# Weight sums of a quad made by accumulating loads, and more quads by seven products, in a decoder layer on one Trainium2 core

## The chip, the core and the metric

One core of a Trainium2 chip runs one launch of the kernel. The core has a matrix engine (TensorE, PE in the profile, with PEld for its weight loads), a vector engine (VectorE, DVE), a scalar engine (ScalarE, ACT), GpSimd (POOL) and SyncE (SP), each with an instruction queue of its own that runs in order, and 16 DMA engines that are shared by all queues that issue loads. The metric is the device time of one launch in microseconds; lower is better. Times are medians of several runs; the profile shows one execution.

## What is computed

One layer of a decoder trunk for 256 rows of 2048 numbers in float32: a modulation by a vector c, a large input projection, two mixers in parallel (a linear recurrence and a sliding-window attention), an output projection, and a SwiGLU feed-forward part with a hidden width of 5632, closed by a norm. The change touches the feed-forward part:

```python
h2 = modulate(rms_norm(x, norm2_g[l]), sh2, sc2)
gate, up = jnp.split(h2 @ w_ffn_in[l], 2, axis=-1)
x = x + g2 * ((jax.nn.silu(gate) * up) @ w_ffn_out[l])
return rms_norm(x, final_g)
```

## The kernel before

**Three products for one.** Every float32 product is taken as three products of rounded parts: each operand is split in a high part (a cast on ScalarE, "hi", line 305) and a low part (the difference on VectorE, "lo", line 317), and `mm3` (lines 353 to 357) issues high x high, high x low and low x high into the same bank. So a weight that was loaded by SP into a "raw" tile costs a cast and a subtraction before TensorE can use it.

**Items and queues.** The weights stream through a list of items, one 128x1024 piece each. `step(i)` (line 327) writes the program order: it issues the load for item i + 5, the high parts up to i + 3, the low parts up to i + 2, extra stages, and then the products of item i. There are five raw tiles, four hi tiles and three lo tiles, so a low part of item i + 2 can only be written after TensorE has finished item i - 1. Work beside the stream (posts, sides) is put between the items by estimated clocks; whatever is written for an engine is run in that order. `Item.before` holds stages that are issued just ahead of an item's products.

**The first FFN projection.** 11 slabs, each 512 columns of the gate half and 512 of the up half; a slab has eight pairs of k-tiles. Slab 0 runs plain, first its gate half (tile names fg), then its up half (fu). In slabs 1 to 10 (`add_pair`, line 1233) a pair of k-tiles, two row halves and two column halves is a 2x2 by 2x2 block product. A plain pair needs eight block products, 24 products of 128x512 with the three parts. A *quad* (`seven`, line 399) does the same with seven block products, 21 products, on sums of blocks: four sums on the side of the activations, made once, and four sums on the side of the weights, made on VectorE for each quad (lines 418, 419, 424, 425) into tiles named "made" or "last". Some of the seven results are shared by several outputs and are combined on VectorE at the end of a slab (`shared`, `gated_rows`). Before the change the pairs at k = 4, 8, 12 are quads (`SEVEN_1`).

**The last projection.** It runs over 44 k-tiles in two column halves, n = 0 and n = 2. In each half, eight pairs of the first 18 are quads (`SEVEN`), taken in turn with plain pairs (`turns`); the rest are plain. `seven_last` (line 1360) issues for each quad a cast "ah" and a difference "al" of the activation sums "fs"; `combined` adds the shared results.

**The gate row.** The second modulation's gate is made as a row: 32 VectorE operations (`ada_rows`, line 688) add products of loaded halves "aw" into "pa", then four TensorE products "pb" (line 694) sum it over the partitions and ScalarE copies it back. It runs as a side; `all_modulations`, a stage ahead of the first item of slab 1, finishes what is left of it. The halves "aw" use two tiles "araw", which in slabs 1 to 10 hold the weight sums.

Of the kernel before, what the change touches and what calls it, by code (L numbers as in the profile page):

```python
# [16 lines left out]
P = 128  # L17
# [26 lines left out]

N_K = 1
# [18 lines left out]
SEVEN = tuple(range(6, 36, 4))  # L64

SEVEN_1, SLAB_7 = (4, 8, 12), 1
EARLY = NH - 2 * N_HOLD

# [6 lines left out]
def hybrid_layer(  # L75
# [8 lines left out]
    hp = ctx.enter_context(tc.tile_pool(name="hp", bufs=1))  # L84
    bp = ctx.enter_context(tc.tile_pool(name="bp", bufs=N_B4))
# [13 lines left out]
    def b4(name, dt=F32, shape=(4, S)):  # L99
        used["b4"] += 1  # L100
        return bp.tile([P, *shape], dt, tag="b4", name=name)

# [174 lines left out]

    items = []
    live = {}
    at = {"load": 0, "made": 0, "hi": 0, "lo": 0}  # L280

    def do_load(i):
        src, cols = items[i].src, items[i].cols
        if callable(src):
            live[i] = [None, None, None, 0.0]
            return
        raw = wp.tile([P, CH], F32, tag="raw", name=f"raw{i}", bufs=AHEAD - 1)
        nc.sync.dma_start(raw[:, :cols], src)
        live[i] = [raw, None, None, load_time(cols)]

    def do_made(i):
        src = items[i].src
        if callable(src):
            clock["dve"] = max(clock["dve"], live[i - 1][3])
            live[i][0] = src(i)
            charge(1.2, 0)
            live[i][3] = clock["dve"]
# [29 lines left out]
    def step(i):  # L327
# [7 lines left out]
        if items[min(i + N_LO, len(items)) - 1].keep:  # L335
            run_posts()
        for stage in it.before:
# [58 lines left out]

    SUMS = 4

    def seven(loads, where, act, bank, begin, end, made_in, post=None):

        got = {}

# [8 lines left out]
        def block(k, n):  # L411
            l, c0 = where[k, n]
            return got[l][:, c0:c0 + 512]

        def first(i):
            got.update({0: live[i - 2][0], 1: live[i - 1][0]})
            x = got["x"] = made_in(0)
            nc.vector.tensor_tensor(x[:, 0:512], block(0, 1), block(0, 0), op=ALU.subtract)
            nc.vector.tensor_tensor(x[:, 512:], block(0, 1), block(1, 1), op=ALU.subtract)
            return x  # L420

        def second(i):
            y, x = made_in(1), got["x"]
            nc.vector.tensor_tensor(y[:, 0:512], block(1, 1), x[:, 0:512], op=ALU.subtract)
            nc.vector.tensor_tensor(y[:, 512:], block(1, 0), y[:, 0:512], op=ALU.subtract)
            return y

        plain = ((0, (0, 0), "p"), (1, (1, 0), "00"), (6, (1, 1), "01"))
        for l in range(2):
            jobs = [(a, where[kn][1], to) for a, kn, to in plain if where[kn][0] == l]  # L430
            cs = [c0 for _, c0, _ in jobs]
            items.append(Item(
                loads[l], CH, products(*jobs), weight=0.25 * len(jobs), used=(min(cs), max(cs) + 512),
            ))
        items.append(Item(first, CH, products((3, 0, "r"), (5, 512, "u")), weight=0.5))
        items.append(Item(second, CH, products((4, 0, "q"), (2, 512, "10")), post, weight=0.5))

    def sums_of(to, a11, a12, a21, a22):

        s1, s2, s3, s4 = (to[:, i, :] for i in range(SUMS))  # L440
        nc.vector.tensor_tensor(s1, a21, a22, op=ALU.add)
        nc.vector.tensor_tensor(s3, a21, a11, op=ALU.subtract)
        nc.vector.tensor_tensor(s2, s1, a11, op=ALU.subtract)
        nc.vector.tensor_tensor(s4, a12, s2, op=ALU.subtract)
# [63 lines left out]
    h_both = hp.tile([P, NK, 2, S], F32R, tag="h", name="h_both")  # L508
    h_hi, h_lo = h_both[:, :, 0, :], h_both[:, :, 1, :]

    def hact(kt):
# [4 lines left out]
        return h_hi[:, kt, :], h_lo[:, kt, :]  # L516
# [17 lines left out]
    def h_low(kt):  # L534
        nc.vector.tensor_tensor(h_lo[:, kt, :], hx[kt], f32(h_hi[:, kt, :]), op=ALU.subtract)
        h_done.add(kt)

    def modulated():
        for kt in range(2):
# [6 lines left out]
            nc.scalar.copy(h_hi[:, kt, :], hx[kt])  # L546
            yield 0.33, 0
            h_low(kt)
        for kt in range(2, NK):
# [6 lines left out]
            nc.scalar.copy(h_hi[:, kt, :], hx[kt])  # L556
# [540 lines left out]
    def second_norm(banks):  # L1097
        sides[:] = [ada_ffn]
        clock["slack"] = SLACK[1]
        both = h2["both"] = hp.tile([P, NK, 2, S], F32R, tag="h", name="h2_both")  # L1100
        hh, hl = both[:, :, 0, :], both[:, :, 1, :]
# [38 lines left out]
        def high(p):  # L1140
            for j in range(2):
                kt = 2 * p + j
                nc.scalar.activation(hh[:, kt, :], x1T[p][:, j, :], AF.Identity, bias=modc[:, 3, kt:kt + 1])

        def low(p):
            for j in range(2):
                kt = 2 * p + j
                nc.vector.scalar_tensor_tensor(
                    hl[:, kt, :], x1T[p][:, j, :], modc[:, 3, kt:kt + 1], f32(hh[:, kt, :]),
# [42 lines left out]
    def h2act(kt):  # L1192
        return h2["both"][:, kt, 0, :], h2["both"][:, kt, 1, :]
# [21 lines left out]
    def f_parts(s, pts):  # L1215
        if 4 * s + 2 not in SEVEN:
# [4 lines left out]

        fc, fs = b4(f"fc{s}", F32R, (2, 2, S)), b4(f"fs{s}", F32, (8, P))
        nc.scalar.copy(fc[:, 0], pts[0])
        nc.scalar.copy(fs[:, 0:2, :], pts[1][:, :, 0:P])
        nc.scalar.copy(fs[:, 2, :], pts[1][:, 1, P:])
        yield 0, 1.3
        nc.vector.tensor_tensor(fc[:, 1], pts[0], f32(fc[:, 0]), op=ALU.subtract)
        sums_of(fs[:, 3:7, :], fs[:, 0, :], fs[:, 1, :], pts[1][:, 0, P:], fs[:, 2, :])
        free(m=2)
        f_hi[s], f_lo[s], f_sum[4 * s + 2] = fc[:, 0], fc[:, 1], fs  # L1230
        yield 1.5, 0

    def add_pair(s):
# [24 lines left out]
        def shared():  # L1258
# [9 lines left out]
            nc.vector.tensor_tensor(x[:, 1, :], banks["r"], g[:, 1, :], op=ALU.add)  # L1268
            nc.vector.tensor_tensor(x[:, 0, :], banks["r"], x[:, 0, :], op=ALU.add)
# [19 lines left out]
        for k in range(0, NK, 2):  # L1289
            loads = [w_f1[s + 11 * n][:, k * 512:(k + 2) * 512] for n in range(2)]  # L1290
            if k in SEVEN_1:
                last = k == SEVEN_1[-1]
                seven(
                    loads, {(0, 0): (0, 0), (1, 0): (0, 512), (0, 1): (1, 0), (1, 1): (1, 512)}, act(k), bank,
                    k == SEVEN_1[0], last,
# [406 lines left out]
```

## Time and profile before

| | |
|---|---|
| median of 3 runs | 1551.02 us (1550.64 to 1556.88) |
| the profiled execution | 1549.47 us, of which the span from the first to the last instruction is 1547.7 |
| granted TensorE clock, mean | 0.997 |
| slab 0 of the first FFN projection | from 836.8 us of the span |
| slab 1 | from 884.1 us |
| last projection begins | about 1308 us |
| DMA queue of SP | 397.39 MB, 74.5% of 16 engines |
| DMA queue of GpSimd (software) | 1.06 MB |

A profile row names the line, the engine, the operation, the tile written and the tiles read, the shape, the count, then busy time and mean nanoseconds, and after the bar the idle time of the engine just before, with what ended it. In a timeline or chain row the first number is the start in the span and the second the duration. A busy TensorE is counted from modelled ends, so its products overlap: one takes some 390 ns and the next follows after some 227.

### The profile page before, as it was taken

The numbers are of one execution on the slowest core, as the hardware profiler recorded it, in microseconds if no ns is written. First come the engines' busy times: TensorE is split into PE (matmuls) and PEld (weight loads), VectorE is DVE, ScalarE is ACT, GpSimd is POOL, SyncE is SP. The second block draws the span as 40 slices with busy tenths as digits, with TensorE's granted clock in tenths as the row PEclk, the third lists the DMA queues.
The fourth block names the chain that finished last, engine by engine and source line by source line (L and its number), as shares of the span: only waits on it lengthen the run. The fifth ranks groups of instructions, "written<-read, shape, count | busy, mean of one in ns | idle before, by whom it ended". The sixth has DMA issues, their size and how long they took to land.

```text
span 1547.7 us, 22116 instructions
## 1 busy us (share of the span) xinstructions
PE 1530.9 (99%) x8013; PEld 1314.2 (85%) x8013; DVE 1392.2 (90%) x1854; ACT 858.2 (55%) x1113; POOL 3.7 (0%) x11
## 2 busy tenths in 40 slices
PE   8999999999999999999999999999999999999997
PEld 7999999998878887888888788888888888888786
DVE  7889989889888887988988899999999999998998
ACT  4654443776855445444545655555555556664664
POOL 0000000000000000000000000000000000000000
PEclk9999999999999999999999999999999999999999
DMA  9999998666887797999999665565555666766563
GB/s 367 343 320 345 341 315 291 212 203 208 270 275 264 259 328 274 368 339 339 366 384 346 191 202 187 194 198 200 200 192 200 207 193 236 251 206 204 189 212 128
DMA packets 112909, 400.37 MB, mean 259 GB/s; under 512 B 12432, under 2 KB 12576, under 8 KB 112416
## 3 DMA queue, kind: packets, MB, share of 16 engines
q1 hardware_dynamic: 112192, 397.39, 74.5%
q8 instruction: 62, 1.02, 0.3%
q0 software_dynamic: 320, 1.06, 0.2%
q10 hardware_dynamic: 288, 0.52, 0.1%
q14 instruction: 47, 0.39, 0.1%
HBM read 394.72 MB, written 4.20 MB: 258 GB/s over the span
## 4 chain that ended last, share of the span: by engine, by line
PE 93%; DMA 4%; DVE 2%; issue 1%; ACT 0%; SPq 0%; DVEq 0%; ACTq 0%
PE pf L1352 9%; PE f L356 7%; PE f L357 7%; PE f L355 7%; PE wi L357 6%; PE wi L355 6%; PE wi L356 6%; PE wga L357 2%; PE wga L355 2%; PE wga L356 2%; PE wa L357 2%; PE wa L355 2%; PE wa L356 2%; PE wl L356 2%; PE wl L357 2%; PE wl L355 2%
## 5 line engine op out<-in xcount | busy, mean ns | idle before, releaser
L305 ACT CAST hi<-raw 128x1024 fp32r<-128x1024 f32 (+1 forms) x540 | 536.9, 1002 | 447.3 <-PE wi L356 77.2
L317 DVE TENSOR_TENSOR lo<-raw,hi 128x1024 fp32r<-128x1024 f32 (+1 forms) x540 | 618.7, 1159 | 66.0 <-issue 35.0
L357 PE MATMUL wi<-h_both,lo 128*128 128x256 f32 x800 | 227.3, 284 | 3.6 <-DVE lo L317 3.6
L355 PE MATMUL wi<-h_both,hi 128*128 128x256 f32 x800 | 228.0, 285 | 0.0
L356 PE MATMUL wi<-h_both,hi 128*128 128x256 f32 x800 | 227.0, 284 | 0.0
L355 PE MATMUL f<-hi,h_both 128*128 128x512 f32 x460 | 180.2, 392 | 0.0
L357 PE MATMUL f<-hi,h_both 128*128 128x512 f32 x460 | 179.0, 389 | 0.0
L356 PE MATMUL f<-lo,h_both 128*128 128x512 f32 x460 | 179.0, 389 | 0.0
L357 PEld LDWEIGHTS wi<-h_both,lo 128*128 128x128 f32 x800 | 154.2, 193 | 4.0 <-DVE lo L317 4.0
L356 PEld LDWEIGHTS wi<-h_both,hi 128*128 128x128 f32 x800 | 154.3, 193 | 0.2
L355 PEld LDWEIGHTS wi<-h_both,hi 128*128 128x128 f32 x800 | 154.3, 193 | 0.2
L305 ACT CAST hi<-made 128x1024 fp32r<-128x1024 f32 x60 | 63.4, 1057 | 112.8 <-PE f L357 111.3
L496 DVE CUSTOM_DVE_ANT_0 aw<-aw,crow,vec 128x1024 f32<-128x1024 f32 x79 | 100.6, 1278 | 6.2 <-DMA aw<-in_ada_t_dram 6.2
L496 DVE CUSTOM_DVE_ANT_0 aw<-aw,crow,modc 128x1024 f32<-128x1024 f32 x79 | 100.9, 1280 | 3.0 <-DMA aw<-in_ada_t_dram 2.8
L357 PEld LDWEIGHTS f<-hi,h_both 128*128 128x128 f32 x460 | 86.3, 188 | 18.0
L355 PEld LDWEIGHTS f<-hi,h_both 128*128 128x128 f32 x460 | 86.4, 188 | 17.8 <-issue 0.2
L356 PEld LDWEIGHTS f<-lo,h_both 128*128 128x128 f32 x460 | 86.4, 188 | 17.8 <-issue 0.2
L317 DVE TENSOR_TENSOR lo<-made,hi 128x1024 fp32r<-128x1024 f32 x60 | 73.4, 1225 | 25.9 <-PE f L356 20.7
L1352 PE MATMUL pf<-hi,fc 128*128 128x512 f32 x256 | 71.0, 389 | 0.0
L305 ACT CAST hi<-last 128x1024 fp32r<-128x1024 f32 x32 | 33.7, 1054 | 52.5 <-PE pf L1352 49.2
L1352 PEld LDWEIGHTS pf<-hi,fc 128*128 128x128 f32 x256 | 48.1, 188 | 10.0
L355 PE MATMUL wl<-hi,yh 128*128 128x512 f32 x128 | 52.5, 410 | 0.0
(355 smaller groups left out, 2940.4 us busy)
## 6 DMA issues: line engine op xcount, KB each, us to landing
raw<-in_w_f_dram SPq DMA_DIRECT2D x176, 512.0 KB, 4.2
raw<-in_w_in_dram SPq DMA_DIRECT2D x164, 512.0 KB, 7.1
aw<-in_ada_t_dram SPq DMA_DIRECT2D x158, 512.0 KB, 6.5
raw<-in_w_f2a_dram SPq DMA_DIRECT2D x44, 512.0 KB, 4.3
raw<-in_w_f2d_dram SPq DMA_DIRECT2D x36, 512.0 KB, 3.4
raw<-in_w_lru_dram SPq DMA_DIRECT2D x32, 512.0 KB, 6.5
raw<-in_w_att_dram SPq DMA_DIRECT2D x32, 512.0 KB, 7.8
raw<-in_w_o_dram SPq DMA_DIRECT2D x32, 512.0 KB, 8.3
```

Source lines behind the costliest of these rows:

```text
L305: nc.scalar.copy(hi[:, cs], live[i][0][:, cs])
L317: nc.vector.tensor_tensor(lo[:, cs], raw[:, cs], f32(hi[:, cs]), op=ALU.subtract)
L355: nc.tensor.matmul(ps, lhsT=lh, rhs=rh, start=start, stop=False, skip_group_check=True)
L356: nc.tensor.matmul(ps, lhsT=lh, rhs=rl, start=False, stop=False, skip_group_check=True)
L357: nc.tensor.matmul(ps, lhsT=ll, rhs=rh, start=False, stop=stop, skip_group_check=True)
L496: nc.vector.tensor_tensor_reduce(out=r, in0=r, in1=crow[:, j * CH:(j + 1) * CH], op0=ALU.mult, op1=ALU.add, scale=1.0, scalar=dst if j els ...
L1352: nc.tensor.matmul(bank(t, n), lhsT=l[:, rows(t)], rhs=w[:, c0:c0 + 512], start=kt == 0 and k == 0, stop=kt == (EARLY - 2 if (t, n) == (1, ...
```

## The change

Two of a quad's four weight sums are no longer made on VectorE. GpSimd issues two *fill* loads of the same block into both halves of a tile "wx", and later two *adding* loads that add another block to each half while loading. VectorE makes the other two sums, "wy", from these (two operations instead of four). Signs are changed to make the additions possible. SP loads only the part of a block pair that a quad uses directly (three blocks of 256 KB instead of four). Fills are issued 11 items ahead, adds 8. With that, a slab has four quads instead of three (two in slab 10), in the order plain, plain, quad, quad, plain, quad, quad, plain; each half of the last projection has ten instead of eight, in the order of `TURNS`. `all_modulations` moves seven items ahead, so that "araw" is free for the fills. The activations h, the rows of the last norm and their gains move from one large tile into tiles of the pool "b4", which grows by eight.

```diff
+N_H = 8
...
-SEVEN = tuple(range(6, 36, 4))
-
-SEVEN_1, SLAB_7 = (4, 8, 12), 1
+
+N_SUM = (11, 8)
+SEVEN = (6, 10, 12, 14, 18, 22, 24, 26, 30, 34)
+
+SEVEN_1, SLAB_7, LAST_7 = (4, 6, 10, 12), 1, 2
+
+TURNS = "--77-77-77-77-77--"
 EARLY = NH - 2 * N_HOLD
+
+ALL_M = 7
...
-    hp = ctx.enter_context(tc.tile_pool(name="hp", bufs=1))
-    bp = ctx.enter_context(tc.tile_pool(name="bp", bufs=N_B4))
+    bp = ctx.enter_context(tc.tile_pool(name="bp", bufs=N_B4 + N_H))
...
+    def do_sum(j):
+        def do(i):
+            if items[i].sums is not None:
+                items[i].sums[j]()
+                load_time(CH)
+        return do
...
+        upto("fill", do_sum(0), i + N_SUM[0])
+        upto("add", do_sum(1), i + N_SUM[1])
...
+        def fill():
+            x = got["x"] = wp.tile([P, CH], F32, tag="araw", name="wx", bufs=N_ADA)
+            for j in range(2):
+                nc.gpsimd.dma_start(x[:, j * 512:(j + 1) * 512], block(0, 1))
+
+        def add():
+            for j in range(2):
+                nc.gpsimd.dma_start(got["x"][:, j * 512:(j + 1) * 512], block(j, j), accum_op=ALU.add)
 
         def first(i):
-            got.update({0: live[i - 2][0], 1: live[i - 1][0]})
-            x = got["x"] = made_in(0)
-            nc.vector.tensor_tensor(x[:, 0:512], block(0, 1), block(0, 0), op=ALU.subtract)
-            nc.vector.tensor_tensor(x[:, 512:], block(0, 1), block(1, 1), op=ALU.subtract)
-            return x
+            return got["x"], 0
 
         def second(i):
-            y, x = made_in(1), got["x"]
-            nc.vector.tensor_tensor(y[:, 0:512], block(1, 1), x[:, 0:512], op=ALU.subtract)
-            nc.vector.tensor_tensor(y[:, 512:], block(1, 0), y[:, 0:512], op=ALU.subtract)
-            return y
+            def raw(*kn):
+                l, c0 = where[kn]
+                return live[i - 3 + l][0][:, c0:c0 + 512]
+
+            y = b4("wy", F32, (CH,))
+            free(b4=1)
+            nc.vector.tensor_tensor(y[:, 0:512], got["x"][:, 0:512], raw(1, 1), op=ALU.add)
+            nc.vector.tensor_tensor(y[:, 512:], y[:, 0:512], raw(1, 0), op=ALU.add)
+            return y, 1.3
...
-        for k in range(0, NK, 2):
+        sevens = SEVEN_1 if s < 10 else SEVEN_1[:LAST_7]
+        others = [k for k in range(0, NK, 2) if k not in sevens]
+        for k in others[:2] + list(sevens[:2]) + others[2:3] + list(sevens[2:]) + others[3:]:
...
         if s == SLAB_7:
-            items[start].before.append(all_modulations)
+            items[start - ALL_M].before.append(all_modulations)
...
-            hi = parts[0] = wp.tile([P, 8, P], F32R, tag="araw", name=f"ah{n}_{k}", bufs=N_ADA)
+            hi = parts[0] = b4(f"ah{n}_{k}", F32R, (8, P))
...
-        others = [k for k in range(0, EARLY, 2) if k not in SEVEN]
-        turns = others[:2] + [k for two in zip(SEVEN, others[2:]) for k in two]
+        kinds = {"7": iter(SEVEN), "-": iter(k for k in range(0, EARLY, 2) if k not in SEVEN)}
+        turns = [next(kinds[c]) for c in TURNS]
```

VectorE, in the up half of slab 0, where the gate row is finished ("lo" a split of the weights, "pa" the gate row, "hs" sums of the activations). Before:

```order
L317 TENSOR_TENSOR lo_8376<-raw_8313,hi_8353 128x1024
L688 SCALAR_TENSOR_TENSOR pa<-aw_8015,cact,pa 128x1024
L317 TENSOR_TENSOR lo_8399<-raw_8333,hi_8374 128x1024
L688 SCALAR_TENSOR_TENSOR pa<-aw_8036,cact,pa 128x1024
L441 TENSOR_TENSOR hs_8414<-x1T_8168 128x128
```

And with the change:

```order
L339 TENSOR_TENSOR lo_8387<-raw_8324,hi_8364 128x1024
L721 SCALAR_TENSOR_TENSOR pa<-aw_8019,cact,pa 128x1024
L339 TENSOR_TENSOR lo_8410<-raw_8344,hi_8385 128x1024
L721 SCALAR_TENSOR_TENSOR pa<-aw_8040,cact,pa 128x1024
L721 SCALAR_TENSOR_TENSOR pa<-aw_8079,cact,pa 128x1024
L721 SCALAR_TENSOR_TENSOR pa<-aw_8190,cact,pa 128x1024
L721 SCALAR_TENSOR_TENSOR pa<-aw_8224,cact,pa 128x1024
L721 SCALAR_TENSOR_TENSOR pa<-aw_8251,cact,pa 128x1024
L721 SCALAR_TENSOR_TENSOR pa<-aw_8303,cact,pa 128x1024
L475 TENSOR_TENSOR hs_8442<-x1T_8179 128x128
```

The last six operations on pa, which stood between splits and sums up to the end of slab 0, now stand in one block.

TensorE, where the gate row's products pb stand, with the last rows of the item ahead and the first of the one behind. Before, between the up half of slab 0 (fu) and slab 1 (f):

```order
L356 MATMUL fu_0_1_8379<-lo_8484,h_both 128x512
L357 MATMUL fu_0_1_8379<-hi_8461,h_both 128x512
L694 MATMUL pb_8553<-pa,ones 128x512
L694 MATMUL pb_8556<-pa,ones 128x512
L694 MATMUL pb_8559<-pa,ones 128x512
L694 MATMUL pb_8562<-pa,ones 128x512
L355 MATMUL f_1_8565<-hi_8482,h_both 128x512
```

And with the change, behind the first of the eight items of the up half:

```order
L380 MATMUL fu_0_1_8390<-lo_8348,h_0_8093 128x512
L381 MATMUL fu_0_1_8390<-hi_8326,h_0_8093 128x512
L727 MATMUL pb_8418<-pa,ones 128x512
L727 MATMUL pb_8421<-pa,ones 128x512
L727 MATMUL pb_8424<-pa,ones 128x512
L727 MATMUL pb_8427<-pa,ones 128x512
L379 MATMUL fu_0_0_8389<-hi_8346,h_1_8094 128x512
```

The four products have moved ahead of seven items.

VectorE, one quad of the last projection ("al" the low part of its activation sums). Before:

```order
L418 TENSOR_TENSOR last<-raw_13241 128x512
L419 TENSOR_TENSOR last<-raw_13241,raw_13253 128x512
L317 TENSOR_TENSOR lo_13284<-raw_13241,hi_13267 128x512
L1370 TENSOR_TENSOR al_10_13286<-fs_9359,ah_10_13271 128x896
L424 TENSOR_TENSOR last<-raw_13253,last 128x512
```

And with the change:

```order
L339 TENSOR_TENSOR lo_13615<-raw_13571,hi_13601 128x512
L1422 TENSOR_TENSOR al_12_13617<-fs_9804,ah_12_13605 128x896
L456 TENSOR_TENSOR wy<-wx,raw_13586 128x512
L457 TENSOR_TENSOR wy<-wy,raw_13586 128x512
L339 TENSOR_TENSOR lo_13638<-raw_13586,hi_13613 128x1024
L339 TENSOR_TENSOR lo_13658<-wx,hi_13636 128x1024
L339 TENSOR_TENSOR lo_13665<-wy,hi_13656 128x1024
```

Two of the four sums are gone, and the first of the two left reads the tile wx, which GpSimd's loads fill.

More of the change, by code (lines that the diff above doesn't have):

```diff
@@ L101, in b4, with h_tiles @@
         return bp.tile([P, *shape], dt, tag="b4", name=name)
+    def h_tiles(name):
+        ts = [bp.tile([P, 2, 2, S], F32R, tag="b4", name=f"{name}{i}") for i in range(N_H)]
+        return [[ts[kt // 2][:, kt % 2, i, :] for i in range(2)] for kt in range(NK)]
     def sum_bank(name):
@@ L276, in __init__ @@
             self.used, self.before = slice(*(used or (0, cols))), list(before)
+            self.sums = None
     items = []
     live = {}
-    at = {"load": 0, "made": 0, "hi": 0, "lo": 0}
+    at = {"fill": 0, "add": 0, "load": 0, "made": 0, "hi": 0, "lo": 0}
+    def do_sum(j):
[4 more added lines that the diff above has]
+        return do
     def do_load(i):
@@ L397, in hybrid_layer, with seven @@
     SUMS = 4
-    def seven(loads, where, act, bank, begin, end, made_in, post=None):
+    def seven(loads, block, by_k, act, bank, begin, end, post=None):
         got = {}
+        where = {(k, n): (k, n * 512) if by_k else (n, k * 512) for k in range(2) for n in range(2)}
         def products(*jobs):
@@ L430, in seven @@
             jobs = [(a, where[kn][1], to) for a, kn, to in plain if where[kn][0] == l]
-            cs = [c0 for _, c0, _ in jobs]
+            cs = [where[kn][1] for _, kn, _ in plain if where[kn][0] == l]
+            used = (min(cs), max(cs) + 512)
             items.append(Item(
-                loads[l], CH, products(*jobs), weight=0.25 * len(jobs), used=(min(cs), max(cs) + 512),
+                loads[l][:, slice(*used)], CH, products(*jobs), weight=0.25 * len(jobs), used=used,
             ))
         items.append(Item(first, CH, products((3, 0, "r"), (5, 512, "u")), weight=0.5))
+        items[-1].sums = fill, add
         items.append(Item(second, CH, products((4, 0, "q"), (2, 512, "10")), post, weight=0.5))
@@ L1215, in f_parts @@
     def f_parts(s, pts):
-        if 4 * s + 2 not in SEVEN:
+        seven_ = [j for j in range(2) if 4 * s + 2 * j in SEVEN]
+        if not seven_:
             fh, fl = b4(f"fh{s}", F32R), b4(f"fl{s}", F32R)
```

138 lines of the change are left out of this document (75 added, 63 removed).

## The prediction

> **What bounds the kernel now.** I read the page first: busy time by engine, and the chain of work that ended last.
>
> ```profile
> PE 1530.9 (99%) x8013; PEld 1314.2 (85%) x8013; DVE 1392.2 (90%) x1854; ACT 858.2 (55%) x1113; POOL 3.7 (0%) x11
> ...
> PE 93%; DMA 4%; DVE 2%; issue 1%; ACT 0%; SPq 0%; DVEq 0%; ACTq 0%
> ```
>
> TensorE sets the time, VectorE is close behind, GpSimd is empty. Then the table by stage (columns: window, its length, busy time of PE, PEld, DVE, ACT, POOL, granted clock, DMA share, GB/s): a stretch of the output projections, one slab of the first FFN projection, and a stretch of the last projection.
>
> ```profile
> 600.00:800.00 200.00, 200.00 (x901) 165.26 (x900) 180.63 (x221) 93.74 (x120) 1.70 (x3) 1.00 0.98 350
> 974.86:1017.23 42.37, 42.37 (x193) 35.17 (x192) 39.36 (x49) 24.01 (x28) 0.00 (x0) 1.00 0.59 199
> 1334.00:1396.30 62.30, 62.30 (x277) 51.58 (x276) 60.36 (x68) 40.26 (x44) 0.00 (x0) 1.00 0.62 203
> ```
>
> In both changed stages TensorE has no gap at the full clock. VectorE fills 39.36 of 42.37 us and 60.36 of 62.30. The DMA engines are at about 0.6, and the first row shows that TensorE can be fed without a gap at 350 GB/s and share 0.98. The list of TensorE's waits names only these two in the last projection:
>
> ```profile
> PE pq L356 <- DVE lo L317: 0.2, 1, 0.2
> PE pr L356 <- DVE lo L317: 0.2, 1, 0.2
> ```
>
> So only fewer products, or a new wait, can move the end. The chain gives the price of a product: transposes recur once per slab, and 24-product pieces once per couple of one plain pair and one quad.
>
> ```profile
> 974.86 0.87 PE ft L957 x8
> ...
> 1017.23 0.87 PE ft L957 x8
> ...
> 1324.93 5.44 PE pf L1352 x24
> ...
> 1335.13 5.44 PE pf L1352 x24
> ```
>
> A slab takes 42.37 us, of which 0.87 are transposes; its 183 products take (42.37 - 0.87) / 183 = 0.2268 us each. A couple takes 10.20 us for 24 + 21 products, 0.2267 each; a plain pair is 5.44 us and a quad 4.76.
>
> **Fewer products.** A quad replaces 24 products of 128x512 by 21. Slabs 1 to 9 go from three quads to four, slab 10 from three to two: +8. The last projection goes from eight to ten in each of two column halves: +4. 12 x 3 = 36 products, 36 x 0.2267 = **-8.16 us**, all on the bound engine. Nothing else leaves TensorE.
>
> **The gate row is finished earlier.** VectorE makes the row "pa" in 32 operations, TensorE spreads it over the partitions in "pb". Before, pb stands at the head of slab 1; now it stands seven items earlier, after the first item of the up half of slab 0. Before this place the instructions stand as they did, so this trace dates it (VectorE, then TensorE):
>
> ```profile
> 855.73 2.36 DVE L317 TENSOR_TENSOR lo<-raw,hi 128x1024 fp32r<-128x1024 f32 x2
> 859.31 1.22 DVE L317 TENSOR_TENSOR lo<-raw,hi 128x1024 fp32r<-128x1024 f32 x1 [1.22 <-issue]
> 860.45 1.28 DVE L688 SCALAR_TENSOR_TENSOR pa<-aw,cact,pa 128x1024 f32<-128x1024 f32 x1
> 862.03 1.23 DVE L317 TENSOR_TENSOR lo<-raw,hi 128x1024 fp32r<-128x1024 f32 x1 [0.30 <-ACT x1T L1165]
> 863.17 1.28 DVE L688 SCALAR_TENSOR_TENSOR pa<-aw,cact,pa 128x1024 f32<-128x1024 f32 x1
> 864.37 0.28 DVE L441 TENSOR_TENSOR hs<-x1T 128x128 f32<-128x128 f32 x1
> ...
> 879.65 1.28 DVE L688 SCALAR_TENSOR_TENSOR pa<-aw,cact,pa 128x1024 f32<-128x1024 f32 x1
> ```
>
> ```profile
> 861.77 0.39 PE L357 MATMUL fu<-hi,h_both 128*128 128x512 f32 x1
> 862.00 0.39 PE L355 MATMUL fu<-hi,h_both 128*128 128x512 f32 x1
> ...
> 881.04 3.59 PE L694 MATMUL pb<-pa,ones 128*128 128x512 f32 x8
> ```
>
> Before, the last seven pa operations lie between the splits and end at 880.93; pb follows at 881.04 without a wait. Now six of them stand in one block behind the split of 862.03. That split needs the "lo" tile which the item ending on TensorE at 862.00 gives back (three tiles), so the block cannot begin before 863.17. The first column half of pa is complete after five operations. They follow one another every 1.20 us (863.17 to 864.37), so it is ready at 863.17 + 4 x 1.20 + 1.28 = 869.25. pb stands next in TensorE's queue from 862.0 on, and behind it all products of the up half: **+7.3 us** of an idle TensorE, whose inputs lie ready. Their being ready wins nothing back: no later part is bound by VectorE's lead. The 3.59 us of pb itself are the same as before. From below this wait is 0, if something finishes pa earlier; from above 8.5, if pb waits for the sixth operation too. I take 7.3, as both queues and the release are in these rows.
>
> **VectorE.** Durations in the last stretch:
>
> ```profile
> L317 DVE TENSOR_TENSOR lo<-raw,hi 128x1024 fp32r<-128x1024 f32 x20 | 23.8, 1219 | 0.0
> L418 DVE TENSOR_TENSOR last<-raw 128x512 f32<-128x512 f32 x6 | 4.1, 685 | 0.0
> ```
>
> Back to back an operation costs 0.08 less than its duration (two splits in 2.36 us: 1.14 to the next). A quad loses two of its four sums, 2 x 0.605; an added quad brings three more blocks to split and two sums. In a slab VectorE stays below 39.4 of now 41.7 us: hidden under TensorE. In the last projection the order becomes two quads, one plain pair. Two couples of before cost VectorE 60.36 / 62.30 x 20.40 = 19.76; less one plain pair (2.28) and four sums (2.42) that is 15.06 against TensorE's 2 x 4.76 + 5.44 = 14.96. Five double quads with four plain pairs between them are 73.0 against 69.4. The lead of two items shrinks from plain ones to quad ones (5.4 to 2.7 us) and covers 2.7 of the 3.6 missing, so about 0.9 us is lost in each half. With no lead it would be 3.6, with the spread of before 0: I take **+2** for both halves (0 to 7). ScalarE used 40.26 / 62.30 x 20.40 = 13.2 us in two couples and has less to cast in the new turn: hidden.
>
> **The accumulating loads.** Each quad now needs two fill loads and two adding loads of 256 KB from GpSimd's queue, the adds waiting for the fills, into two tiles in turn. The trace has no adding load; nearest are GpSimd's own loads and SP's.
>
> ```profile
> raw<-in_w_f_dram SPq DMA_DIRECT2D x176, 512.0 KB, 4.2
> ...
> raw<-in_w_f2a_dram SPq DMA_DIRECT2D x44, 512.0 KB, 4.3
> raw<-in_w_f2d_dram SPq DMA_DIRECT2D x36, 512.0 KB, 3.4
> ```
>
> ```profile
> L1021 POOL DMA_DIRECT2D g<-g1d x2: 527/541/555, 727.3 to 727.9; - x2
> ...
> DMA to landing us min/median/max: 5.4/7.2/10.0
> ```
>
> Call F the time from the first fill's issue to the landing of both, A the same for the adds. From SP's rows F = 4.3 + 0.54 for the second issue, about 4.9 at a DMA share of 0.6; from GpSimd's, issued at a share of 0.98, 7.2. A lies between the same ends, plus, if an add occupies the engines for twice its bytes, 0.5 MB / 350 GB/s = 1.5. A tile must do F, A, and then 3.5 us (two sums and two splits) per turn. In the last projection a turn is 14.96 us: **F + A up to 11.5 is hidden**. In a slab, the tile of the third quad comes free 1.2 us after TensorE begins the first quad (one split), and must be full 2.4 us (two sums and a split) before the second item of the third quad, which begins 2 x 4.76 + 5.44 + 1.36 = 16.3 us after the same moment: F + A = 12.7. GpSimd's queue holds fill, add, fill, add in turn, so the fourth quad's fill goes out only 1.2 + F + 1.1 after that moment; its deadline, 4.76 later, leaves 2F + A = 16.4. Three plain pairs in a row then restore the lead. I take F = 4.9 and A = 4.9 + 1.5 = 6.4 (F + A = 11.3, 2F + A = 16.2), since the demand stays short of saturation: a slab moves 44 blocks in 41.7 us, 277 GB/s. So I charge 0, with almost no reserve.
>
> The Trainium skill ("DMA: Bandwidth & Descriptors", Anatomy of one DMA) fits a GpSimd-issued load by 2.0 us plus its bytes over 436 GB/s; as an estimate, two loads of 256 KB together give 3.2, so F + A = 6.4 and no loss at all. The 7.2 us of this trace speak against it, though that was under load.
>
> **Sum.** 1549.47 (the profiled execution; span 1547.7) - 8.16 + 7.3 + 2 + 0 = 1550.6. The median of the runs shown, 1551.02, is 1.55 above that execution, so I forecast 1552.2.
>
> **Rivals.** Half a per cent, 7.8 us, is about what a measurement of this kernel can tell from no change.
>
> - The wait at pb is absent and only the products count: 1551.02 - 8.16 = 1543. For it: the inputs of pa landed long before. Against: both queues are in order. 0.09.
> - The tile is late (slower): the point is F + A = 11.5. At 7.2 + 7.2 each turn in the last projection takes 17.9, which is 2.9 too long, four times in each half: 23 us, 1575; at 12.5 it is 8 us, 1560. For it: two quads in a row put the DMA share near 0.96 (0.62 x 315 / 203), where 7.2 was seen. Against: TensorE waits first, and then demand falls. 0.23. If the slabs are late as well, 1.7 us for two quads in ten slabs add 34.
> - The engines' capacity: a turn moves 18 blocks, 4.72 MB, 315 GB/s; with every add counted twice 22 blocks, 5.77 MB, 385 GB/s. At 350 that takes 16.5 us, 1.5 too long, five times in each half: 15 us, 1567. 0.10. The Trainium skill states on the same page (Rules for kernel authors) that an accumulate reads its destination and writes it later; no run here shows what that costs.
>
> The forecast has the other 0.58. The range runs from 1546 to 1575: it leaves out the first rival (0.09) and the late slabs (about 0.08). Faster 0.09, within 0.58, slower 0.33 (both later rivals lie above 1558.8).
>
> **What would show it.** pb right after the first item of slab 0's up half, with a TensorE gap near 7.3 us before it; slabs of 42.37 - 0.68 = 41.69 us; two quads and a plain pair in 14.96; waits for "wx" on ScalarE and VectorE of about nothing. The forecast is wrong if pb does not wait, if slabs stretch over 42, or if the turn in the last projection follows the loads rather than 14.96.

## The result and the profile after

The change makes the kernel slower: 1602.62 us median against 1550.83, ratio 1.0334 [1.0307, 1.0361]; a second set of runs of the same kernel, the first of the experiments below, gave 1607.93 against 1551.80, 1.0366 [1.0334, 1.0397]. One of the four runs of the first set took 2566.84 us at a mean granted clock of 0.556, and one with plain loads below 2185.38 us at 0.654; the medians and ratios here leave these two out (with its run the first median is 1605.11). All rows of "after" are from a profiled execution of the second set (1611.21 us, span 1609.4).

The page after: TensorE has 36 products fewer, as counted, but its busy share falls from 99 to 96%, and loads of the sum tile "wx" stand in the chain that ended last.

```profile
PE 1546.9 (96%) x7977; PEld 1312.7 (82%) x7977; DVE 1382.7 (86%) x1825; ACT 877.4 (55%) x1146; POOL 172.5 (11%) x243
...
PE 77%; DMA 14%; DVE 4%; issue 2%; ACT 2%; POOL 1%; SPq 0%; DVEq 0%; ACTq 0%; POOLq 0%
DMA wx<-in_w_f_dram 7%; PE wi L381 6%; PE wi L379 6%; PE wi L380 6%; PE pf L1404 6%; PE f L379 5%; PE f L380 5%; PE f L381 4%; DMA wx<-in_w_f2d_dram 3%; DVE lo L339 3%; DMA wx<-in_w_f2a_dram 2%; PE wl L380 2%; PE wga L381 2%; PE wga L379 2%; PE wga L380 2%
```

Where the time went can be dated by the first and the last transposes "ft" of the slabs, in TensorE's timeline of before and of after.

```profile
889.95 1.03 PE L957 MATMUL ft<-ident,sg 128*128 128x128 f32 x8
...
1313.68 1.03 PE L957 MATMUL ft<-ident,v 128*128 128x128 f32 x8
```

```profile
901.77 1.03 PE L990 MATMUL ft<-ident,sg 128*128 128x128 f32 x8
...
1351.15 1.03 PE L990 MATMUL ft<-ident,v 128*128 128x128 f32 x8
```

Up to the first transposes after has lost 11.8 us; the ten slabs take 449.4 us instead of 423.7, 25.7 more; from there to the end of the span it is 258.2 against 234.0, 24.2 more. Since the 24 products fewer in the slabs should have saved 5.4 and the 12 fewer in the last projection 2.7, the losses are about 31 and 27 us. Two slabs and two stretches of the last projection by stage, and the list of TensorE's waits:

```profile
992.79:1041.36 48.57, 45.23 (x191) 36.10 (x189) 39.27 (x47) 25.40 (x30) 11.69 (x16) 0.93 0.82 239
1041.36:1085.47 44.11, 42.46 (x191) 34.39 (x189) 38.69 (x50) 25.20 (x31) 11.67 (x16) 1.00 0.88 261
1352.19:1438.32 86.13, 77.89 (x331) 62.70 (x331) 75.56 (x81) 54.24 (x62) 27.27 (x38) 0.98 0.91 272
1481.84:1567.34 85.50, 74.53 (x307) 58.80 (x307) 73.91 (x78) 52.05 (x58) 23.19 (x32) 0.96 0.84 243
```

```profile
PE pf L380 <- DVE lo L339: 18.9, 10, 3.4
PE f L380 <- DVE lo L339: 9.5, 9, 2.1
PE pb L727 <- DVE pa L721: 7.1, 1, 7.1
PE fr L380 <- DVE lo L339: 6.7, 10, 0.8
```

Before, TensorE stood without a gap in both stages. Now no engine is full there: TensorE waits 7.1 us once for the gate row (pb, in slab 0), 16.2 us in the slabs (f, fr) and 18.9 us in the last projection (pf) for low parts "lo". Where the gaps are long, the granted clock is under 1 as well (0.93 and 0.96), which adds to the loss. What the low parts wait for stands in the chain that ended last. This is its piece in the slab of 44.11 us (start, duration, engine, tile):

```profile
1052.69 1.83 DVE lo L339 x2
...
1054.81 5.78 DMA wx<-in_w_f_dram
...
1060.88 0.77 POOL wx L444
1061.65 7.64 DMA wx<-in_w_f_dram
1069.39 1.05 ACT hi L327
```

VectorE gives the sum tile back at 1054.52 with its split for the second quad; the fill goes out at once, the adds follow when the fill has landed, and ScalarE can cast the fourth quad's sums at 1069.39. The chain has such a piece in eight of the ten slabs. In the last projection ScalarE waits 23.9 us for sum tiles and VectorE 5.0. The loads say why the tiles are late (the fill loads, then the adding loads; "landing" is from issue to arrival):

```profile
L440 POOL DMA_DIRECT2D wx<-in_w_f_dram x76: 541/567/1125, 866.3 to 1296.1; - x76
...
DMA to landing us min/median/max: 2.8/5.9/9.7
```

```profile
L444 POOL DMA_DIRECT2D wx<-in_w_f_dram x76: 877/896/1240, 870.2 to 1304.4; - x76
...
DMA to landing us min/median/max: 3.8/6.6/9.9
```

Two fills take 0.57 + 5.9, about 6.5 us, and two adds 0.90 + 6.6, about 7.5: F + A = 14.0 us, beyond the limits of 11.5 and 12.7 that the prediction had worked out. In the piece above they take 14.8 (1054.52 to about 1069.3): 2.1 more than 12.7, in a slab that is 2.4 us longer than 41.7.

### The profile page after: what moved, and what is told of

It reads as the page before. It is cut to its first block, busy times and chain, and to the rows that moved or that the text cites. A ratio compares the mean times of both kernels' runs of the same rounds, so it can differ in the third digit from the quotient of the medians.

```text
span 2565.0 us, 22494 instructions
## 1 busy us (share of the span) xinstructions
PE 2547.5 (99%) x7977; PEld 1665.5 (65%) x7977; DVE 1416.1 (55%) x1825; ACT 898.4 (35%) x1146; POOL 172.9 (7%) x243
## 4 chain that ended last, share of the span: by engine, by line
PE 99%; DVE 0%; issue 0%; ACT 0%; DMA 0%; DVEq 0%; ACTq 0%
PE pf L1404 8%; PE f L379 7%; PE f L380 7%; PE f L381 7%; PE wi L380 6%; PE wi L379 6%; PE wi L381 6%; PE wl L380 2%; PE wga L379 2%; PE wa L379 2%; PE wgl L379 2%; PE wa L381 2%; PE wgl L380 2%; PE wo L381 2%; PE wgl L381 2%; PE wo L380 2%
## 5 line engine op out<-in xcount | busy, mean ns | idle before, releaser
L379 PE MATMUL wi<-h,hi 128*128 128x256 f32 x800 | 307.7, 385 | 0.0
L381 PE MATMUL wi<-h,lo 128*128 128x256 f32 x800 | 306.8, 384 | 0.0
L380 PE MATMUL wi<-h,hi 128*128 128x256 f32 x800 | 306.3, 383 | 0.0
L379 PE MATMUL f<-hi,h 128*128 128x512 f32 x412 | 239.2, 581 | 0.0
L380 PE MATMUL f<-lo,h 128*128 128x512 f32 x412 | 237.7, 577 | 0.0
L381 PE MATMUL f<-hi,h 128*128 128x512 f32 x412 | 236.7, 574 | 0.0
L379 PEld LDWEIGHTS wi<-h,hi 128*128 128x128 f32 x800 | 233.0, 291 | 1.4 <-issue 0.8
L380 PEld LDWEIGHTS wi<-h,hi 128*128 128x128 f32 x800 | 232.7, 291 | 1.3 <-issue 0.6
L381 PEld LDWEIGHTS wi<-h,lo 128*128 128x128 f32 x800 | 232.9, 291 | 0.1
L339 DVE TENSOR_TENSOR lo<-wx,hi 128x1024 fp32r<-128x1024 f32 x58 | 71.1, 1226 | 116.1 <-PE f L380 53.4
L381 PEld LDWEIGHTS f<-hi,h 128*128 128x128 f32 x412 | 90.8, 220 | 67.2 <-issue 37.0
L380 PEld LDWEIGHTS f<-lo,h 128*128 128x128 f32 x412 | 91.0, 221 | 66.4 <-issue 38.3
L379 PEld LDWEIGHTS f<-hi,h 128*128 128x128 f32 x412 | 89.8, 218 | 67.9 <-issue 39.6
L339 DVE TENSOR_TENSOR lo<-wy,hi 128x1024 fp32r<-128x1024 f32 x58 | 71.1, 1225 | 49.1 <-PE f L380 39.9
```

Source lines behind the costliest of these rows:

```text
L339: nc.vector.tensor_tensor(lo[:, cs], raw[:, cs], f32(hi[:, cs]), op=ALU.subtract)
L379: nc.tensor.matmul(ps, lhsT=lh, rhs=rh, start=start, stop=False, skip_group_check=True)
L380: nc.tensor.matmul(ps, lhsT=lh, rhs=rl, start=False, stop=False, skip_group_check=True)
L381: nc.tensor.matmul(ps, lhsT=ll, rhs=rh, start=False, stop=stop, skip_group_check=True)
```

## The experiments

Three theories stood at first. **Theory 1**: the tile is late, because two tiles in turn don't give fill, wait and add enough time. **Theory 2**: the 16 DMA engines are full, with the adds counted twice. **Theory 3**: VectorE is too full in the last projection. The runs' edits are against the changed kernel unless said; the kernel before gave medians of 1551.7 to 1552.8 us beside them.

**The change again.**

> The changed kernel as it is, for a profile at the full clock. Theory 1 (the sum tile wx comes too late: fill, wait, add, and only two tiles): TensorE waits some 7 us for the gate row and in all some 45 us for splits of wx and wy, in the slabs (about 43 to 45 us each instead of 41.7) and in the turns of the last projection (16 to 18 us instead of 15.0); SP's own loads land as before (4 to 5 us) and ScalarE waits for wx, not for raw. Theory 2 (the DMA engines are full): the DMA share is above 0.95 in the slabs, SP's loads land in 7 us or more and ScalarE waits for raw as much as for wx. Theory 3 (VectorE is full in the last projection): VectorE has no idle time in the turns and the loss lies there alone.

1607.93 us; its rows are those above. Slabs take 43.2 to 48.6 us and turns 16.9 to 18.7, with ScalarE waiting for wx, as theory 1 had it, at a share of 0.82 to 0.88 in the two slabs shown; but SP's loads land later too (a median of 5.1 us in the slabs and 6.7 in the first half of the last projection, against 4.2 and 4.3 before).

**Plain loads in place of the adding ones** (the weight sums are not computed), in two runs:

```diff
-                nc.gpsimd.dma_start(got["x"][:, j * 512:(j + 1) * 512], block(j, j), accum_op=ALU.add)
+                nc.gpsimd.dma_start(got["x"][:, j * 512:(j + 1) * 512], block(j, j))
```

> The second loads of each quad no longer add, they overwrite the first (so the two weight sums are not computed). Same bytes from HBM, same queues, same waits. Theory 1, with the add as the long part: the second loads land as fast as the fills and most of the loss goes: about 1565 us or less. Theory 2: if an add counts twice in the engines, the time falls as well, with the DMA share; if not, it stays near 1603. Theory 3: stays near 1603.

> The change with plain loads in the place of the accumulating ones, once more for a profile at the full clock (the weight sums are not computed). If the accumulating load itself is what takes long, the second loads land in the time of the fills, 5.9 us or less, and GpSimd issues them in 0.57 us instead of 0.90, so F + A falls from 14 to about 12 and slabs to about 42.5. If GpSimd's queue or the full engines make both long, the second loads take 6.6 us here too.

1572.33 us, 1.0134 [1.0116, 1.0151], and 1573.02 in the single later run: 35 us of the loss go with the addition alone, somewhat less than theory 1 had expected. The fills, the second loads, and a slab of the later run:

```profile
L440 POOL DMA_DIRECT2D wx<-in_w_f_dram x76: 536/538/543, 865.1 to 1269.8; - x76
...
DMA to landing us min/median/max: 2.7/4.3/7.3
```

```profile
L444 POOL DMA_DIRECT2D wx<-in_w_f_dram x76: 536/538/547, 869.1 to 1276.5; - x76
...
DMA to landing us min/median/max: 2.8/4.8/7.4
```

```profile
1070.70:1112.67 41.97, 41.97 (x189) 34.45 (x188) 38.46 (x47) 25.48 (x30) 8.56 (x16) 1.00 0.79 276
```

Without the addition a pair of fills takes 4.3 + 0.54 = 4.84 us, almost exactly the F = 4.9 of the prediction, and the second pair 5.3: together 10.2, under both limits, and slabs come down to between 42.0 and 43.1 (eight full ones; 42.4 on average). The addition makes the second loads longer by 1.8 us in landing and 0.36 in GpSimd's issue of each, and it makes the fills beside them longer too, by 1.6. The turns of the last projection still take mostly 16.1 us here, though its tiles come in time.

**Three sum tiles instead of two** (a third 4 KB tile, one tile fewer in the ring b4):

```diff
-AHEAD, N_HI, N_LO, N_ADA, N_B4 = 6, 4, 3, 2, 25
+AHEAD, N_HI, N_LO, N_ADA, N_B4 = 6, 4, 3, 3, 25
...
-    bp = ctx.enter_context(tc.tile_pool(name="bp", bufs=N_B4 + N_H))
+    bp = ctx.enter_context(tc.tile_pool(name="bp", bufs=N_B4 + N_H - 1))
...
-                if self.own < N_ADA:
+                if self.own < 2:
```

> Three tiles for wx instead of two (the gate row's halves still use two of them; the pool b4 has one tile less). A fill need no longer wait for the quad before last. Theory 1: the turn per tile grows by half, so the loss beyond the gate row's wait mostly goes: 1555 to 1565 us. Theory 2 and theory 3: near 1603.

1569.66 us, 1.012 [1.0103, 1.0137], above the 1555 to 1565 expected. The adds land as late as before (6.6 us), but the slabs take 42.0 to 42.1 us (transposes at 1022.77 and 1064.84) and the waits "f" are gone but for 0.2 us: in the slabs theory 1 is shown. The last projection stays long; its turn of two quads and a plain pair takes 16.8 us instead of 14.96 in the first half, and 16.1 to 17.5 in the second.

Some 5 us of what this run gains on the change lie ahead of the first FFN projection, where no quad is at work. The first product of that projection starts at 833.2 us, in the change at 838.4; in all runs with three tiles it starts between 831.8 and 833.5, in those with two, the kernel before included, between 836.8 and 838.4. No run tells why.

**The old counts and order with the accumulating loads** (three quads in a slab, eight in each half of the last projection, in turn with plain pairs):

```diff
-SEVEN = (6, 10, 12, 14, 18, 22, 24, 26, 30, 34)
+SEVEN = tuple(range(6, 36, 4))
-SEVEN_1, SLAB_7, LAST_7 = (4, 6, 10, 12), 1, 2
+SEVEN_1, SLAB_7, LAST_7 = (4, 8, 12), 1, 3
-TURNS = "--77-77-77-77-77--"
+TURNS = "--7-7-7-7-7-7-7-7-"
...
-        for k in others[:2] + list(sevens[:2]) + others[2:3] + list(sevens[2:]) + others[3:]:
+        for k in range(0, NK, 2):
```

> The accumulating loads with the old numbers and the old order of quads (three per slab at k = 4, 8, 12, eight per half, always with a plain pair between two quads). 36 more products than the change: +8.2 us. Theory 1: a tile's turn is 20.4 us (two couples) and fill plus add fit in it: 1551 + 7 = about 1558 us, the wait for the gate row alone. Theory 2: three quarters of the extra bytes: about 1590. Theory 3: VectorE has 2 x 0.6 us less per quad than in the kernel before: about 1558.

1561.85 us, 1.006 [1.0043, 1.0078]. A slab, two couples of the last projection, and its wait at pb:

```profile
1070.11:1112.48 42.37, 42.37 (x193) 35.18 (x191) 36.02 (x43) 23.99 (x28) 8.77 (x12) 1.00 0.85 255
1354.73:1375.13 20.40, 20.40 (x92) 16.90 (x91) 17.61 (x20) 13.06 (x15) 5.83 (x8) 1.00 0.93 283
```

```profile
870.40 5.87 PE L727 MATMUL pb<-pa,ones 128*128 128x512 f32 x8 [7.13 <-DVE pa L721]
```

Slabs and couples take the 42.37 and 20.40 us of before, so in both stages the accumulating loads as such cost nothing when quads stand apart, at 283 GB/s and a share of 0.93; VectorE even does with 17.61 us where it had 19.76. Nearly all of the loss that is left stands at pb, in a wait of 7.13 us and products that then take 5.87 instead of 3.59; these 2.3 us were not in the 1558 expected.

**Four quads in the slabs, the last projection in its old order, two tiles** (only the lines SEVEN and TURNS of the diff above):

> The change, but the last projection again with eight quads that alternate with plain pairs (the old order); the slabs keep four quads. Two sum tiles, as in the change. Theory 1 (with two sum tiles, fills and adds of two quads in a row are not done in time, F + A about 14 us against limits of 12.7 in a slab): the slabs are long again, 43.8 to 48.6 us, and the waits for the tile stay there, about 31 us more than nine slabs of 41.7; the last projection is as before, couples of 10.2 us. Sum: before 1551.8 + 7.1 (pb) - 10 slabs x 0.68 + 31 = 1583, 1578 to 1590. Theory 2 (DMA engines full): much of the loss comes from the last projection's two adjoining quads, so under 1570. If the slabs alone make the loss, 1600 or more.

1586.08 us, 1.0221 [1.0201, 1.024]. As theory 1 had it: the slabs are long again (ten take 449 us), so they lose by themselves, TensorE waits nowhere in the last projection, and theory 2's account, in which most of the loss comes from the adjoining quads there, falls.

**The last projection: three tiles, its rows loaded later.** In the run with three tiles VectorE's timeline showed a wait in each turn of the first half:

```profile
1362.99 0.69 DVE L456 TENSOR_TENSOR wy<-wx,raw 128x512 f32<-128x512 f32 x1 [0.57 <-PE pf L380]
```

The second sum "wy" of the second quad waits for a tile of the ring b4 that TensorE still reads for the first quad, and what is behind it on VectorE waits too. (The run with plain loads, which has the tile more in this ring, does not show this wait.) So the rows x2 and fg, which hold three tiles of that ring for each half, were loaded late:

```diff
-                last_first()
-                sides.append(Side(fetch_last()))
+                last_first()
+            if jobs[0][0] == ROWS_AT and jobs[0][1] in (0, 2):
+                sides.append(Side(fetch_last(jobs[0][1] // 2)))
...
+ROWS_AT = 20
```

> Three sum tiles (as in the run with three), and the rows x2 and fg of the last projection, three 4 KB tiles for each half, are loaded at k-tile 20 of their half instead of at its beginning, so that up to then three to six more tiles of the ring b4 are free there. Nothing else moves. Theory A (in the run with three tiles the turn of two quads and a plain pair took 16.77 us instead of 14.96 because the second quad's sum tile wy, from the ring b4, waits for the end of the first quad, which reads the tile ah: VectorE stands, and with it the split of the next plain block): turns of 15.0 to 15.2 us up to k-tile 20, 1569.7 - 8 turns x 1.7 = about 1556, 1553 to 1559. Theory B (VectorE or the DMA engines are full at two quads and a plain pair, 281 GB/s with each add counted once): turns stay at 16.5 to 16.8, 1568 to 1571.

1567.42 us, 1.0099 [1.0083, 1.0115]: a miss for theory A, mostly. The wait is gone, but the turn only falls to 16.1 us. One turn of VectorE, ScalarE and TensorE (single lines), and two turns by stage:

```profile
1355.52 1.23 DVE L340 TENSOR_TENSOR lo<-wx,hi 128x1024 fp32r<-128x1024 f32 x1 [0.69 <-issue]
1357.05 1.23 DVE L340 TENSOR_TENSOR lo<-wy,hi 128x1024 fp32r<-128x1024 f32 x1 [0.30 <-ACT hi L328]
```

```profile
1353.20 1.06 ACT L328 CAST hi<-wx 128x1024 fp32r<-128x1024 f32 x1 [1.66 <-PE pf L1403]
1355.96 1.06 ACT L328 CAST hi<-wy 128x1024 fp32r<-128x1024 f32 x1 [1.71 <-PE pf L1403]
```

```profile
1354.82 0.61 PE L1403 MATMUL pf<-lo,fc 128*128 128x512 f32 x2
```

```profile
1346.28:1362.40 16.12, 15.27 (x66) 12.31 (x67) 15.06 (x17) 10.94 (x13) 5.79 (x8) 1.00 0.96 279
...
1378.55:1394.65 16.10, 15.25 (x66) 12.31 (x66) 15.05 (x17) 10.94 (x13) 4.32 (x6) 1.00 1.03 364
```

VectorE is busy 15.06 us of each turn, the predicted figure, and idle for 1.0. While TensorE does the plain pair (its two pieces last 2.72 us each), buffers come back slowly, and VectorE waits twice. The wait of 0.69 us is not for a cast: the cast of wx ended at 1354.26. It ends at 1355.52, just after the last products that read the plain pair's second low part (1354.82 + 0.61), so what is missing there is a lo tile, of which there are three. The wait of 0.30 is for the cast of wy, which itself had waited 1.7 us for a hi tile. 15.06 + 1.0 is the turn. The second row is the turn in which the rows were loaded as well: 364 GB/s, and the same length. So the DMA engines don't set it, and theory 2 and theory B's DMA part fall. Theory 3 holds for the last projection, in the form that VectorE's work and its waits fill the turn. In the second half the late rows cost a step of 4.1 us: VectorE waits 3.2 us and ScalarE 6.3 for a sum tile whose loads went out among theirs.

**pb at the head of slab 1, on top of that** (`row_made` finishes pa; `all_modulations` then issues pb):

```diff
...
-            items[start - ALL_M].before.append(all_modulations)
+            items[start - ALL_M].before.append(row_made)
+            items[start].before.append(all_modulations)
```

> As the run before it, and the gate row pa is still finished seven items early, but its four products pb go out at the head of slab 1, as in the kernel before; so TensorE's wait of 7.1 us at pb should be gone. Expected: 6 to 7 us less than the run with the rows later: 1549 by theory A (1546 to 1552), 1563 by theory B. If pb's wait was covered by another wait right behind it, the two runs are equal.

1563.52 us (1556.33 to 1569.35), 1.0071 [1.0045, 1.0098]. The wait at pb is gone, and all slabs start 4.5 us earlier (1017.32 instead of 1021.84), not 6 to 7: in its place TensorE waits 2.0 us once for a low part of slab 0 ("fu"), and the next products run at half the pace for some 3 us. The spread of these runs is as large as the gain; the slab starts show it, the medians alone would not. The profiled execution lost the gain again in the last projection, where the late rows cost steps of 4.7 and 3.9 us.

**A fifth buffer for the high halves** (from the ring b4, with the rows loaded one by one at k-tiles 16, 20 and 28):

```diff
-            hi = wp.tile([P, CH], F32R, tag="hi", name=f"hi{i}", bufs=N_HI)
+            hi = wp.tile([P, CH], F32R, tag="hi", name=f"hi{i}", bufs=N_HI + 1)
...
-    bp = ctx.enter_context(tc.tile_pool(name="bp", bufs=N_B4 + N_H - 1))
+    bp = ctx.enter_context(tc.tile_pool(name="bp", bufs=N_B4 + N_H - 2))
```

> The run with the rows later and pb later, with a fifth buffer for the high halves hi (taken from the ring b4, 31 tiles), and the rows x2 and fg of each half loaded one by one at k-tiles 16, 20 and 28. Theory C (in the run with the rows later, the turn took 16.12 us because VectorE, 15.06 us busy in it, waited 1.0 us for casts that ScalarE could not make before the plain pair's products gave their hi buffer back; the DMA engines have room, since a turn with 364 GB/s lasted 16.10 us): turns of 15.1 to 15.3 us, no step of 4 us at the rows, 1563.5 - 10 x 0.9 - 5 = about 1549, 1546 to 1553. Theory D (the turn is bound by DMA or by something else): turns stay at 16.1, 1557 to 1560.

1557.63 us, 1.0042 [1.0027, 1.0057], between the ranges of the two theories. The turn falls to 15.7 us (second quads at 1335.70, 1351.44, 1367.15), about half of what theory C had expected. The wait for the cast is gone and the one of 0.69 us is left: VectorE's split of wx begins at 1344.95, 4 us after its cast, when the last products that read the plain pair's low part have ended (1344.24 + 0.61). So hi tiles were the smaller part and lo tiles, by this trace, are the rest; no run with a fourth lo tile tried it. TensorE still waits 1.7 to 3.2 us at three places of the last projection, so the time is 8 us above the 1549 of theory C. The slabs now take 41.72 us (1013.96 to 1055.68), the 41.69 of the prediction, which had stood at 42.0 with four hi buffers.

**Quads in the slabs only, three tiles, pb at the head of slab 1.** The edits for three tiles, for the old SEVEN and TURNS and for pb together; then also the fifth hi buffer and the late rows:

> Four quads in each slab with three sum tiles, pb at the head of slab 1, and the last projection with the old eight quads that alternate with plain pairs. Slabs of 42.0 us instead of 42.37 as in the run with three tiles, no wait at pb, couples of 10.20 us: 1552.8 - 10 x 0.37 = 1549, 1546 to 1552. If the lead that the wait at pb gave VectorE is missed in the next slab, 1 to 3 us more.

> The run with quads in the slabs only, three sum tiles and pb at the head of slab 1, with the fifth hi buffer and the last projection's rows loaded one by one at k-tiles 16, 20 and 28. With the fifth buffer the slabs took 41.72 us instead of 42.0 (ten quads in the last projection, then); with couples of 10.20 us as before in the last projection: 1547.2 - 10 x 0.3 = 1544, 1542 to 1548. If the rows loaded late hold up a sum tile, as they did at ten quads (steps of 1.7 to 3.2 us at three places), 1548 to 1550.

1547.17 us, 0.997 [0.996, 0.9979], and 1543.99 us, 0.9955 [0.994, 0.9969]: both faster than the kernel before by less than 1%, the second by 7.8 us, and both within the range expected. Not all of it is the quads': in the second run's trace the first transposes come 1.1 us earlier than before, the ten slabs take 420.2 us instead of 423.7, and the rest 0.9 less. A stretch of 42 us in the slabs (which take 41.72 us here) and a piece of the last projection in it have no gap:

```profile
1050.00:1092.00 42.00, 42.00 (x191) 34.74 (x191) 38.61 (x47) 25.27 (x30) 11.61 (x16) 1.00 0.92 276
...
1330.40:1350.80 20.40, 20.40 (x92) 16.89 (x91) 17.70 (x19) 13.05 (x14) 5.84 (x8) 1.00 0.97 281
```

## Why the prediction was wrong

The forecast was 1552.2 us, the range ended at 1575, and the chance of the right side was 0.33.

- **The accumulating loads: the step that failed.** "I take F = 4.9 and A = 4.9 + 1.5 = 6.4 (F + A = 11.3, 2F + A = 16.2)", and then "So I charge 0, with almost no reserve". With adds F is 6.5 and A 7.5. The runs agree with the limits: 10.2 us (plain second loads) frees most of the slabs, 14.0 doesn't, and one tile more, which moves the limits and not the loads, frees them as well. It was the tile's turn (12.7) that bound, by 2.1 us in the piece of the chain above, and not GpSimd's queue (2F + A = 16.4): the late fill went out as soon as the tile was free. The extra 1.5 for an add was not far off (2.2 measured, issue and landing), but I gave the fills the value of a stage without adds, and they slow down beside adds by 1.6 us. The plain loads of GpSimd at a share of 0.98, 7.2 us, were the nearer row: demand was said to stay "short of saturation" by GB/s, while the share in the slabs rose to 0.88. Cost: about 31 us in the slabs and some 13 in the last projection. The 6.4 us that the prediction worked out from the Trainium skill ("DMA: Bandwidth & Descriptors", Anatomy of one DMA) lie further off on the same side; even the plain pairs took 10.2.
- **VectorE in the last projection: right in its busy time, wrong in its price.** 15.06 us for a turn came out to the digit. "about 0.9 us is lost in each half" did not: I set VectorE's work against TensorE's and let a lead cover the rest, as if VectorE never waited. In each turn it waits 0.69 us for a lo tile and 0.30 for a cast, both because TensorE gives buffers back late during the plain pair, and pays it ten times: 1.15 x 10 = 11.5 us where the term was 2 and its upper end 7, with the tiles in time. The run with plain loads, where the tiles come in time, shows the shares: from the last transposes to the end it takes 245.5 us, some 14 more than 234.0 less the 2.7 of the products. So about half of the 27 us there stays with VectorE when the tiles come in time, and the other half, 13, goes with the addition.
- **pb: right in place and size, with a term missing.** 7.3 us forecast, 7.13 measured, at that place. But after the gap pb's own products took 5.4 to 6.5 us instead of 3.59 in the runs that had the wait, in after at a granted clock of 0.50 to 0.61. "The 3.59 us of pb itself are the same as before" was wrong by 2 to 3 us. "No later part is bound by VectorE's lead" was not quite so either: without the wait at pb TensorE waits 2.0 us further on in slab 0. In after, 7.1 + 2.9 are 10.0 of the 11.8 us lost up to the first transposes; nearly all of the other 1.8 lie ahead of slab 0, which begins 1.6 later.
- **The products: right.** 36 fewer; 41.72 us for a slab once nothing else holds it, 41.69 forecast.
- **The rivals.** The late tile is what happened, in its stronger form: 1575 and, "if the slabs are late as well", 34 more make 1609, close to the measured time. Part of that may be luck: in the last projection that sum had the late tiles alone, while half of the 27 us there stay when the tiles come in time, and some 3 us at pb were missing in it. That form was left out of the range with about 0.08. The engines' capacity as the bound falls by the turn at 364 GB/s; its premise, that an add counts twice, is borne out below.

## What to carry to other kernels

A load chain with a wait inside it (fill, wait, add) must fit between the release of its buffer and its use, under the loads it adds itself: take its time from a row at the share that the change will bring, with one buffer more where the reserve is thin. An engine with 15.06 us of work in a turn of 14.96 is not 0.1 us late per turn if it also waits for an engine that the turn slows down: add its waits, by their buffers, before letting a lead cover the rest. Work that is taken off a second-busiest engine pays only as far as the bound engine's own work falls, so put it where the slack for the new waits is (here the slabs with three tiles, not the last projection).

## What the runs showed of the hardware

**An adding load occupies the DMA engines about twice.** Slabs of equal length and bytes, with plain second loads (0.79 at 276 GB/s, above) and with adding ones in the run with quads in the slabs only:

```profile
1058.96:1101.02 42.06, 42.06 (x190) 34.46 (x189) 38.38 (x47) 25.53 (x30) 11.73 (x17) 1.00 0.92 276
```

The difference is 0.92 x 42.06 - 0.79 x 41.97 = 5.5 us of all engines for eight loads of 256 KB (2.1 MB); at the plain slab's 33.2 us for 11.6 MB these bytes take 6.0. So GB/s don't show it, and the share does.

**The granted clock can fall after short gaps too.** Stretches behind gaps of TensorE of 7.13 us (after), 4.13 us (the run with the rows later) and 1.96 us (the fifth hi buffer):

```profile
870.90:874.00 3.10, 3.10 (x4) 1.50 (x5) 2.03 (x5) 0.58 (x1) 2.21 (x4) 0.50 0.72 98
874.00:877.40 3.40, 3.40 (x6) 1.34 (x5) 0.00 (x0) 1.17 (x2) 0.00 (x0) 0.61 0.80 202
```

```profile
1517.90:1524.00 6.10, 6.03 (x15) 4.68 (x16) 4.74 (x5) 4.82 (x5) 0.00 (x0) 0.53 0.34 102
```

```profile
1386.00:1390.00 4.00, 4.00 (x13) 3.16 (x13) 3.25 (x3) 3.82 (x5) 2.00 (x3) 0.69 0.84 193
```

Columns are as in the tables by stage; the granted clock is the third number from the end. A clock between 0.5 and 1 is a mean: behind the gap of 1.96 us eight products follow every 0.43 us instead of 0.227, about half the pace, and then the old pace is back. That gap so costs nearly twice its length, and this is part of why TensorE's waits in after sum to less than the loss. But the length does not decide it. Behind a gap of 1.99 us (the run with the rows later) the clock stayed at 1.00:

```profile
1466.31 0.50 PE L381 MATMUL pf<-lo,ah 128*128 128x512 f32 x1 [1.99 <-DVE lo L340]
```

```profile
1466.30:1474.00 7.70, 7.69 (x34) 6.33 (x35) 7.67 (x9) 5.15 (x6) 2.90 (x4) 1.00 0.85 217
```

The wait of 2.0 us for "fu" is at the same place in all four runs with pb at the head of slab 1: in two of them half the pace follows for about 3 us, in the two with the fifth hi buffer it does not. Behind the regular single gaps of 0.46 to 1.51 us in the runs with three tiles it stayed at 1.00. The Trainium skill ("TensorE: Matmul & The Clock Gate", Part 1: The HAM clock gate) puts the fall to half the clock at an idle window of about 3.4 us that runs freely; the gaps of 4.13 and 7.13 us agree, and the one of 1.96 us, shorter than that, was followed by the fall here too.
